# Long convolutions of a Hyena layer: packed outer stages, another order of partition rows, stores on SyncE's queue, loads asked for earlier

## The chip, the cores and the metric

One core of one Trainium2 chip runs the whole program. The metric is the device time of one execution in microseconds (us). Of the kernel before, three executions were timed; one further execution was recorded by the hardware profiler.

## What is computed

The reference is a two-layer backbone over 1024 latent tokens of width 1024 (and 256 context tokens). Layer 0 mixes tokens with a gated linear recurrence, layer 1 with an order-2 Hyena operator; each is followed by a squared-ReLU MLP with 4096 hidden units. The change lies in the Hyena operator of layer 1 alone, which cut to its core is:

```python
def long_conv(u, k_f, bias):
    L = u.shape[1]
    u32 = u.astype(jnp.float32)
    y = jnp.fft.irfft(jnp.fft.rfft(u32, n=2 * L, axis=1) * k_f, n=2 * L, axis=1)[:, :L]
    return (y + u32 * bias).astype(u.dtype)

def hyena_operator(u, p, conv_fn):
    ...
    z = conv_fn(u @ w_in + b_in, conv_w, conv_b, HYENA_CONV_LEFT)
    v, x1, x2 = jnp.split(z, HYENA_ORDER + 1, axis=-1)
    k_f = hyena_filters(L, fw1, fb1, fw2, fb2, fw3, fb3, fw4, freq)
    v = x1 * long_conv(v, k_f[:, 0], skip[0])
    v = x2 * long_conv(v, k_f[:, 1], skip[1])
    return v @ w_out + b_out
```

So there are a projection to three streams with a short convolution along rows of 64 tokens, two long circular convolutions with gates between, and a projection back.

## The kernel before

All work is float32. Weights of the big projections are split into a high and a low part, and three matmuls at a quick format stand for one (L154, L135 to L137). The long convolutions use plain float32 matmuls, which the trace shows as two MATMUL instructions each.

**Projection stage.** `in_gemm` makes 24 blocks of 128 channels. `use` adds the bias (ACT, L888) and does the short convolution (DVE, L894 to L896) for each half of the tokens; `finish`, three blocks later, transposes the blocks of `v` and `x1` (PE, L923; ACT, L924) into `V` and `X1`, or sends a block of `x2` to DRAM (L908).

**The transform.** A long convolution over 1024 tokens padded to 2048 is done as a transform in two stages. The outer forward stage `s1` takes one slice `g` of 8 of `V` and makes two row blocks with two matmuls against `m1` (L864); ACT copies each from PSUM to a tile `e` (L866), and a DMA stores `e` (128 partitions) into 8 partitions of `BIG` (L868), all 16 blocks of them. `prow` says which partitions a row block has. So the stores turn the data by a quarter: `BIG[:, f]` then has all rows of frequency block f on its partitions. Stores are issued by ACT inside the main loop, by SP before it.

**The main loop.** There are four units: two convolutions by two halves of the channels. Each has 16 steps, one for each frequency block. `fstep` loads the filter block `ft` from DRAM (SP, L970), transforms it (PE, L974; ACT copy `kk`, L976), transforms the signal (PE, L979), multiplies them as complex numbers (four DVE operations on half the partitions each, L983 to L986, and for block 0 three small ones more, L989 to L991), and lets POOL add the two products into `y` (L993). `bstep`, three steps later (`LAG`), transforms `y` back (PE, L998) and ACT copies the result over `BIG[:, f]` (L999).

**The outer inverse stage.** `s2p` undoes the outer stage for one slice g: SP loads two row blocks of `BIG` into tiles `e` (L957, pool tag `e2` with six buffers), PE multiplies each by `md` into one PSUM tile (L958), and DVE multiplies by `X1` (L962) or ACT copies (L964) into `V`. The stages `s2p` of unit u-1 and `s1` of unit u+1 ride beside the steps of unit u as a list `side`; from step 4 to step 12 about two entries of it follow each step. In the last unit `back`, which transposes four slices to channels (L1015) and multiplies by `x2` (L1016), takes the place of `s1`.

**Order.** In the main loop `pin` fixes the order of PE's matmuls as written. Elsewhere, and on the other engines, a scheduler that runs with the build sets the order. A wait of an instruction holds back all that stand behind it on the same engine; on SP and ACT that goes for DMA issues too.

**The output projection** follows: `load` fetches weights `hy_w_out`, `gemm2` takes 24 matmuls for each block of 128 channels, and `s2p(3, ...)` and `back(4)` to `back(7)` stand between them.

## Time and profile before

| | |
|---|---|
| Timed executions | 2819.17 us median of 3 (2819.03 to 2819.62) |
| Profiled execution, its own time | 2820.53 us |
| Its span in the profile | 2818.8 us, 30100 instructions |
| PE busy (matmul) | 2664.5 us, 95% of the span |
| DVE, ACT, POOL busy | 1519.5, 1045.7, 256.6 us |

PE is TensorE, DVE VectorE, ACT ScalarE, POOL GpSimd, SP SyncE, which issues most DMAs. PE's share of the span is an average over stages: in most of them it never stops, in the main loop it does.

### The profile page before, as it was taken

The numbers are of one execution on the slowest core, as the hardware profiler recorded it, in microseconds if no ns is written. First come the engines' busy times: TensorE is split into PE (matmuls) and PEld (weight loads), VectorE is DVE, ScalarE is ACT, GpSimd is POOL, SyncE is SP. The second block draws the span as 40 slices with busy tenths as digits, with TensorE's granted clock in tenths as the row PEclk, the third lists the DMA queues.
The fourth block names the chain that finished last, engine by engine and source line by source line (L and its number), as shares of the span: only waits on it lengthen the run. The fifth ranks groups of instructions, "written<-read, shape, count | busy, mean of one in ns | idle before, by whom it ended". The sixth has DMA issues, their size and how long they took to land. (4 is left out here: it accounts for less than half of the span.)

```text
span 2818.8 us, 30100 instructions
## 1 busy us (share of the span) xinstructions
PE 2664.5 (95%) x11578; PEld 2027.9 (72%) x11578; DVE 1519.5 (54%) x2077; ACT 1045.7 (37%) x1566; POOL 256.6 (9%) x162
## 2 busy tenths in 40 slices
PE   6689898999999999999999998889799999999998
PEld 1577777878777777778787763333588888888887
DVE  7665665874554554554843447547485333333336
ACT  5557577552333333322622233323353221112213
POOL 0223333010000000000100013212000000000000
PEclk8789999999999999999999999999999999999999
DMA  8331122342443443431313235555421111111112
GB/s 302 124 123 40 50 75 100 117 129 75 135 134 114 142 133 110 135 114 57 120 56 111 83 123 150 139 162 160 134 83 48 51 47 51 45 53 45 53 45 97
DMA packets 120272, 286.28 MB, mean 102 GB/s; under 512 B 11898, under 2 KB 27900, under 8 KB 120002
## 3 DMA queue, kind: packets, MB, share of 16 engines
q1 hardware_dynamic: 109618, 261.30, 29.5%
q10 hardware_dynamic: 8256, 14.68, 1.8%
q0 software_dynamic: 2256, 8.39, 0.9%
q8 instruction: 91, 1.49, 0.2%
q14 instruction: 51, 0.42, 0.0%
HBM read 212.76 MB, written 37.75 MB: 89 GB/s over the span
## 5 line engine op out<-in xcount | busy, mean ns | idle before, releaser
L154 PE MATMUL ps<-u,whi 128*128 128x512 f32 x2696 | 733.5, 392 | 0.0
L115 ACT CAST whi<-raw 128x1024 fp32r<-128x1024 f32 x206 | 216.7, 1052 | 1130.8 <-PE ps L154 1033.5
L154 PEld LDWEIGHTS ps<-u,whi 128*128 128x128 f32 x2696 | 504.1, 188 | 114.6 <-DVE x L789 4.2
L117 DVE TENSOR_TENSOR wlo<-raw,whi 128x1024 fp32r<-128x1024 f32 x206 | 262.1, 1272 | 468.7 <-ACT whi L115 467.9
L154 PE MATMUL ps<-u,wlo 128*128 128x512 f32 x1348 | 421.3, 389 | 0.1
L154 PEld LDWEIGHTS ps<-u,wlo 128*128 128x128 f32 x1348 | 252.9, 188 | 53.7 <-DVE wlo L117 0.8
L154 PE MATMUL ps<-hh,whi 128*128 128x512 f32 x896 | 290.6, 393 | 0.0
L154 PE MATMUL ps<-hh,wlo 128*128 128x512 f32 x896 | 288.4, 389 | 0.0
L154 PE MATMUL ps<-hl,whi 128*128 128x512 f32 x896 | 287.7, 390 | 0.0
L154 PEld LDWEIGHTS ps<-hh,whi 128*128 128x128 f32 x896 | 168.2, 188 | 51.4 <-DVE x L789 11.1
L136 PE MATMUL ps<-u,whi 128*128 128x512 f32 (+1 forms) x508 | 195.4, 386 | 3.7 <-POOL u L292 3.1
L135 PE MATMUL ps<-u,whi 128*128 128x512 f32 (+1 forms) x508 | 187.3, 385 | 11.5 <-ACT u L291 11.5
L137 PE MATMUL ps<-u,wlo 128*128 128x512 f32 (+1 forms) x508 | 193.1, 382 | 1.8 <-DVE wlo L117 1.8
L154 PEld LDWEIGHTS ps<-hh,wlo 128*128 128x128 f32 x896 | 168.1, 188 | 35.2
L154 PEld LDWEIGHTS ps<-hl,whi 128*128 128x128 f32 x896 | 167.9, 188 | 33.8
L789 DVE SCALAR_TENSOR_TENSOR big<-ps,mod,big 128x512 f32<-128x512 f32 (+1 forms) x132 | 91.7, 731 | 185.2 <-PE ps L154 177.7
L789 DVE SCALAR_TENSOR_TENSOR x<-ps,mod,x 128x512 f32<-128x512 f32 x128 | 91.4, 747 | 132.8 <-PE ps L154 124.9
L415 DVE TENSOR_TENSOR ht<-ps,ht 128x512 f32<-128x512 f32 x64 | 44.0, 687 | 162.9 <-PE ps L137 162.9
L292 POOL TENSOR_TENSOR u<-nu,u 128x512 fp32r<-128x512 f32 x24 | 33.9, 1412 | 990.6 <-ACT u L291 981.4
L135 PEld LDWEIGHTS ps<-u,whi 128*128 128x128 f32 x508 | 98.0, 194 | 30.1 <-ACT u L291 12.3
L136 PEld LDWEIGHTS ps<-u,whi 128*128 128x128 f32 x508 | 98.2, 193 | 25.6 <-POOL u L292 6.4
L137 PEld LDWEIGHTS ps<-u,wlo 128*128 128x128 f32 x508 | 97.7, 192 | 20.3 <-DVE wlo L117 3.0
(228 smaller groups left out, 3798.2 us busy)
## 6 DMA issues: line engine op xcount, KB each, us to landing
raw<-in_mlp_w_dram SPq DMA_DIRECT2D x136, 512.0 KB
adaw<-in_ada_w_dram SPq DMA_DIRECT2D x112, 256.0 KB
fd<-fe SPq DMA_DIRECT2D x64, 256.0 KB
ft<-fd SPq DMA_DIRECT2D x64, 256.0 KB
e<-big SPq DMA_DIRECT2D x64, 256.0 KB
eraw<-in_ada_w_dram SPq DMA_DIRECT2D x24, 512.0 KB
raw<-in_hy_w_in_dram SPq DMA_DIRECT2D x24, 512.0 KB
big<-e ACTq DMA_DIRECT2D x48, 256.0 KB
```

The costliest lines, as they stand in the source:

```text
L115: lsplit[0] = nc.scalar.copy(hi, raw)
L117: lsplit[1] = nc.vector.tensor_tensor(lo, raw, hi.bitcast(F32), op=ALU.subtract)
L135: first = pin(nc.tensor.matmul(ps, wh, rh, start=start, stop=False))
L136: pin(nc.tensor.matmul(ps, wh, rl, start=False, stop=False))
L137: pin(nc.tensor.matmul(ps, wl, rh, start=False, stop=stop))
L154: nc.tensor.matmul(pp[c], x, y[c][k], start=first, stop=last)
L292: applied[k % 2] = (nc.vector if k % 2 else nc.gpsimd).tensor_tensor(ul[k], u, uh[k].bitcast(F32), op=ALU.subtract)
L415: nc.vector.tensor_tensor(ht, ps, ht, op=ALU.mult)
L789: last[0] = nc.vector.scalar_tensor_tensor(xs[m][:, cs], ps[:, :n], g2[:, m:m + 1], xs[m][:, cs], op0=ALU.mult, op1=ALU.add)
```

## The change

Six things change together.

- `s1` and `s2p` take two slices at a time (`gp`). The zero blocks of `m1` and `md` go, and each full matmul becomes several small ones on different parts of the PE array: `s1` 8 matmuls of 32 rows by 64 columns, `s2p` 8 of 64 rows by 32 columns for a pair of slices, where 4 full ones stood. They write to the two single PSUM tiles `st` and `rb` and, for `s1`, to two of the six shared ones.
- For that, tokens lie in another order: `use` permutes in ACT's read and writes the short convolution in five DVE operations with runs of 8 elements where three stood (for `v` and `x1`), `finish` copies the odd slices by quarters of the partitions, two on ACT and two on DVE, and `back` multiplies by a permutation matrix `pm` as a full float32 matmul where it had a transpose.
- `prow` puts neighbouring row blocks into different halves of the partitions.
- All stores of `s1` are issued by SP. In the loop a fourth buffer for `e` is added.
- `s2load` issues the loads of `s2p` apart from it: those of the first two pairs at step 3, with 12 buffers `e2`. In the output projection it stands right ahead of `s2p(3, m)`, with 4 buffers.
- `fload` asks for a filter block three steps ahead, with 4 buffers in place of 8, and `kstep` transforms it one step ahead.

```diff
 def prow(g):
-    return 32 * (g >> 2) + (g & 3)
+
+    return 64 * (g & 1) + 32 * (g >> 3) + (g >> 1 & 3)
...
-            def s1(u, g):
+            def s1(u, gp):
...
-                for m in range(2):
-                    ps = psum()
-                    pin(nc.tensor.matmul(ps, m1[:, m], V[c][:, g], start=True, stop=True))
-                    e = bp.tile([P, 512], F32, tag="e", name=nm("e"), bufs=3)
-                    nc.scalar.copy(e, ps)
-                    b = prow(2 * g + m)
-                    (nc.scalar if cp[0] else nc.sync).dma_start(BIG[u][b:b + 29:4], e)
+                pp = [[psum_st(), psum_rb()], [psum(), psum()]]
+                for r in range(4):
+                    rows = slice(32 * r, 32 * r + 32)
+                    for n in range(2):
+                        k = 3 - r if n else r
+                        pin(nc.tensor.matmul(pp[n][k // 2][64 * (k % 2):64 * (k % 2) + 64], m1[rows], V[c][rows, 2 * gp + n], start=True, stop=True))
+                for n in range(2):
+                    for m in range(2):
+                        if cp[0] and n and m:
+                            e = cp[0].tile([P, 512], F32, tag="e", name=nm("e"), bufs=1)
+                        else:
+                            e = bp.tile([P, 512], F32, tag="e", name=nm("e"), bufs=3)
+                        nc.scalar.copy(e, pp[n][m])
+                        b = prow(4 * gp + 2 * n + m)
+                        nc.sync.dma_start(BIG[u][b:b + 29:4], e)
...
+                    nc.vector.tensor_scalar(ov, zv, cw[:, 1, r:r + 1], cw[:, 3, r:r + 1], op0=ALU.mult, op1=ALU.add)
+                    for tap_, o_, i_ in ((0, ov[:, 1:], zv[:, :7]), (0, ov[:, 0, 1:], zv[:, 7, :7]), (2, ov[:, :7], zv[:, 1:]), (2, ov[:, 7, :7], zv[:, 0, 1:])):
+                        nc.vector.scalar_tensor_tensor(o_, i_, cw[:, tap_, r:r + 1], o_, op0=ALU.mult, op1=ALU.add)
...
-                    nc.scalar.copy(dst[c][:, 4 * g4:4 * g4 + 4, o:o + P], pt.rearrange("p (g d) -> p g d", g=4))
+                    pv = pt.rearrange("p (h n d) -> p n h d", h=2, n=2)
+                    dv = dst[c][:, 4 * g4:4 * g4 + 4, o:o + P].rearrange("p (h n) d -> p n h d", n=2)
+                    nc.scalar.copy(dv[:, 0], pv[:, 0])
+                    for r in range(4):
+                        (nc.scalar.copy if r % 2 else nc.vector.tensor_copy)(dv[96 - 32 * r:128 - 32 * r, 1], pv[32 * r:32 * r + 32, 1])
...
+            def s2load(u, gp, pool=cA, bufs=12):
+
+                ee = rows_[u, gp] = []
+                for n in range(2):
+                    for m in range(2):
+                        e = pool.tile([P, 512], F32, tag="e2", name=nm("e2"), bufs=bufs)
+                        b = prow(4 * gp + 2 * n + m)
+                        nc.sync.dma_start(e, BIG[u][b:b + 29:4])
+                        ee.append(e)
+
+            def s2p(u, gp):
+
                 o, c = units[u]
...
+                po = [psum_st(), psum_rb()]
+                ee = rows_.pop((u, gp))
+                for r in range(2):
+                    rows = slice(64 * r, 64 * r + 64)
+                    for n in range(2):
+                        for m in range(2):
+                            k = 2 * m + r
+                            k = 3 - k if n else k
+                            pin(nc.tensor.matmul(po[n][32 * k:32 * k + 32], md[rows], ee[2 * n + m][rows], start=True, stop=True))
...
+            def fload(i):
+                if i < 64:
+                    fts[i] = cA.tile([P, 512], F32, tag="ft", name=nm("ft"), bufs=4)
+                    nc.sync.dma_start(fts[i], fd[i // 16, FORD[i % 16]])
...
-                        pin(nc.tensor.transpose(pt[:, gg * P:(gg + 1) * P], V[c][:, 4 * g4 + gg, j * P:(j + 1) * P], ident))
+                        pin(nc.tensor.matmul(pt[:, gg * P:(gg + 1) * P], V[c][:, 4 * g4 + gg, j * P:(j + 1) * P], pm[:, gg % 2], start=True, stop=True))
...
+                            def both(u, g):
+                                if g == 0:
+                                    s2load(u, 2)
+                                elif g == 1:
+                                    s2load(u, 3)
+                                s2p(u, g)
+                            side += [lambda g=g, u=u: both(u - 1, g) for g in range(4)]
...
+                    if f == LAG and u:
+                        s2load(u - 1, 0)
+                        s2load(u - 1, 1)
...
                     ys[i] = fstep(u, f)
-                    while len(side) > ns - min(ns, -(-ns * (f - f0 + 1) // (13 - f0))):
+                    fload(i + 3)
+                    if i < 63:
+                        kstep(i + 1)
+                    while len(side) > ns - min(ns, -(-ns * (f - f0 + 1) // (14 - f0))):
```

How the instructions stand is shown at three places. First SP's queue in unit 1, where the row blocks of unit 0 are loaded (L957 before, L990 now, `e`) among the filter blocks (L970 before, L1019 now, `ft`). Before:

```order
L970 DMA ft_12871<-fd 128x512
L957 DMA e_2390_12675<-big_11178 128x1x512
L957 DMA e_2391_12678<-big_11178 128x1x512
L957 DMA e_2394_12684<-big_11178 128x1x512
L957 DMA e_2395_12687<-big_11178 128x1x512
L957 DMA e_2405_12711<-big_11178 128x1x512
L957 DMA e_2406_12714<-big_11178 128x1x512
L970 DMA ft_12910<-fd 128x512
L970 DMA ft_12949<-fd 128x512
L957 DMA e_2408_12719<-big_11178 128x1x512
L957 DMA e_2409_12722<-big_11178 128x1x512
```

The same place of the change, from the sixth of the first run of loads on:

```order
L990 DMA e_2384_12885<-big_11344 128x1x512
L990 DMA e_2385_12887<-big_11344 128x1x512
L990 DMA e_2386_12889<-big_11344 128x1x512
L990 DMA e_2402_12926<-big_11344 128x1x512
L990 DMA e_2403_12928<-big_11344 128x1x512
L990 DMA e_2404_12930<-big_11344 128x1x512
L990 DMA e_2405_12932<-big_11344 128x1x512
L1019 DMA ft_12960<-fd 128x512
L990 DMA e_2417_12966<-big_11344 128x1x512
L990 DMA e_2418_12968<-big_11344 128x1x512
L990 DMA e_2419_12970<-big_11344 128x1x512
L990 DMA e_2420_12972<-big_11344 128x1x512
```

Twelve loads now stand in one run where six stood, one filter block and then the last four follow; the eight filter blocks of steps 0 to 7 are ahead of the run.

Second PE in unit 1, step 4 and after: `s2p` (L958 before, L1004 now), the back transform (L998, now L1055), the filter's (L974, now L1025) and the signal's (L979, now L1036). Before:

```order
L979 MATMUL ps_12664<-big_12181,m_12183 128x512
L958 MATMUL ps_12674<-e_2390_12675,md 128x512
L958 MATMUL ps_12674<-e_2391_12678,md 128x512
L958 MATMUL ps_12683<-e_2394_12684,md 128x512
L958 MATMUL ps_12683<-e_2395_12687,md 128x512
L998 MATMUL ps_12691<-y_12615,mi_12186 128x512
L974 MATMUL ps_12696<-ft_12694,m_12183 128x512
L979 MATMUL ps_12700<-big_12181,m_12183 128x512
```

In the change:

```order
L1025 MATMUL ps_12922<-ft_12866,m_12393 128x512
L1004 MATMUL pst_12934<-e_2379_12875,md 32x512
L1004 MATMUL pst_12934<-e_2380_12877,md 32x512
L1004 MATMUL prb_12935<-e_2381_12879,md 32x512
L1004 MATMUL prb_12935<-e_2382_12881,md 32x512
L1004 MATMUL pst_12934<-e_2379_12875,md 32x512
L1004 MATMUL pst_12934<-e_2380_12877,md 32x512
L1004 MATMUL prb_12935<-e_2381_12879,md 32x512
L1004 MATMUL prb_12935<-e_2382_12881,md 32x512
L1055 MATMUL ps_12947<-y_12845,mi_12396 128x512
L1036 MATMUL ps_12950<-big_12391,m_12393 128x512
L1025 MATMUL ps_12962<-ft_12901,m_12393 128x512
```

Eight small matmuls in a row, which need all four row blocks by the fourth of them, stand where four full ones stood that need one row block each.

Third PE in the output projection (L154 before, L155 now, of `gemm2`), around the third pair of `s2p(3, ...)`. Before:

```order
L154 MATMUL ps_14082<-yh_13976,wlo_14079 128x512
L958 MATMUL ps_14109<-e_2928_14110,md 128x512
L958 MATMUL ps_14109<-e_2929_14113,md 128x512
L958 MATMUL ps_14117<-e_2931_14118,md 128x512
L958 MATMUL ps_14117<-e_2932_14121,md 128x512
L154 MATMUL ps_14125<-yh_13955,whi_14077 128x512
```

In the change:

```order
L1004 MATMUL pst_14431<-e_2927_14423,md 32x512
L155 MATMUL ps_14444<-yh_14264,wlo_14393 128x512
L155 MATMUL ps_14443<-yh_14267,whi_14391 128x512
L1004 MATMUL pst_14431<-e_2928_14425,md 32x512
L1004 MATMUL pst_14431<-e_2927_14423,md 32x512
L1004 MATMUL pst_14431<-e_2928_14425,md 32x512
L1004 MATMUL prb_14432<-e_2929_14427,md 32x512
L155 MATMUL ps_14444<-yh_14270,whi_14391 128x512
L155 MATMUL ps_14443<-v_14247,whi_14391 128x512
L155 MATMUL ps_14444<-v_14247,whi_14391 128x512
L1004 MATMUL prb_14432<-e_2930_14429,md 32x512
```

Here, where no order is fixed, the eight small ones are torn into runs: two runs of four for each of the first two pairs, three runs for the third and four for the fourth, 11 in all.

## Rows read from the trace of the kernel before

**Rows 1.** By stage: length, busy PE, PEld, DVE, ACT, POOL (count), clock, DMA share, GB/s.
```profile
1384.00:1663.00 279.00, 278.46 (x1256) 226.11 (x1255) 119.55 (x174) 82.12 (x129) 8.37 (x9) 1.00 0.21 68
1663.00:1984.00 321.00, 276.53 (x616) 113.85 (x614) 203.28 (x296) 107.99 (x189) 83.82 (x69) 0.95 0.55 160
1984.00:1992.00 8.00, 0.00 (x0) 0.00 (x0) 0.12 (x1) 1.20 (x2) 0.00 (x0) 0.50 0.70 225
1992.00:2056.00 64.00, 63.58 (x259) 46.88 (x260) 33.15 (x43) 26.14 (x36) 0.00 (x0) 0.97 0.39 129
```

**Rows 2.** Timeline of POOL's additions: start, length, operation, idle before and releaser.
```profile
1668.60 1.26 POOL L993 TENSOR_TENSOR y<-t,t 128x512 f32<-128x512 f32 x1 [2.34 <-DVE t L986]
...
1727.82 1.27 POOL L993 TENSOR_TENSOR y<-t,t 128x512 f32<-128x512 f32 x1 [1.55 <-DVE t L986]
1730.65 1.27 POOL L993 TENSOR_TENSOR y<-t,t 128x512 f32<-128x512 f32 x1 [1.56 <-PE ps L974]
...
1777.21 1.27 POOL L993 TENSOR_TENSOR y<-t,t 128x512 f32<-128x512 f32 x1 [10.35 <-DVE t L990]
...
1817.50 1.28 POOL L993 TENSOR_TENSOR y<-t,t 128x512 f32<-128x512 f32 x1 [1.56 <-DVE t L986]
...
1873.59 1.27 POOL L993 TENSOR_TENSOR y<-t,t 128x512 f32<-128x512 f32 x1 [7.45 <-DVE t L990]
...
1912.13 1.27 POOL L993 TENSOR_TENSOR y<-t,t 128x512 f32<-128x512 f32 x1 [1.55 <-DVE t L986]
...
1950.62 1.27 POOL L993 TENSOR_TENSOR y<-t,t 128x512 f32<-128x512 f32 x1 [8.12 <-DVE t L990]
...
1980.17 1.26 POOL L993 TENSOR_TENSOR y<-t,t 128x512 f32<-128x512 f32 x1 [1.56 <-DVE t L986]
```

**Rows 3.** Timeline of SP's loads and of the matmuls that wait for them.
```profile
1730.40 5.76 SPq L957 DMA_DIRECT2D e<-big  x6
...
1734.47 1.10 PE L958 MATMUL ps<-e,md 128*128 128x512 f32 x2 [0.43 <-DMA e<-big]
1736.28 1.12 PE L958 MATMUL ps<-e,md 128*128 128x512 f32 x2 [0.72 <-DMA e<-big]
1738.31 1.10 PE L958 MATMUL ps<-e,md 128*128 128x512 f32 x2 [0.90 <-DMA e<-big]
...
1820.33 5.70 SPq L957 DMA_DIRECT2D e<-big  x6
...
1913.75 5.69 SPq L957 DMA_DIRECT2D e<-big  x6
```

**Rows 4.** Busy time in three short stretches (columns as in rows 1).
```profile
1668.00:1680.00 12.00, 11.36 (x27) 4.51 (x25) 8.71 (x13) 2.93 (x5) 5.06 (x4) 1.00 0.98 350
...
1732.00:1738.00 6.00, 4.26 (x9) 1.17 (x7) 5.86 (x9) 1.17 (x2) 2.54 (x2) 1.00 0.54 144
...
2002.00:2006.00 4.00, 4.00 (x20) 3.30 (x19) 1.17 (x2) 4.00 (x6) 0.00 (x0) 1.00 0.52 192
```

**Rows 5.** Chain that ended last, in the output projection: start, length, what.
```profile
2009.03 3.43 PE ps L958 x8
...
2048.39 0.87 PE ps L1015 x8
```

**Rows 6.** Timeline of PE in the filter stage, small matmuls among full ones.
```profile
913.68 1.09 PE L432 MATMUL ps<-ht,mf 32*32 32x512 f32 x16
...
914.70 0.50 PE L154 MATMUL ps<-hh,whi 128*128 128x512 f32 x1
```

**Rows 7.** Timeline of ACT's copies ahead of the stores, unit 1.
```profile
1787.66 0.59 ACT L866 COPY e<-ps 128x512 f32<-128x512 f32 x1 [1.44 <-DMA big<-e]
1789.64 0.59 ACT L866 COPY e<-ps 128x512 f32<-128x512 f32 x1 [1.39 <-DMA big<-e]
```

**Rows 8.** Timeline of the first store of unit 0 and the transfer ahead of it.
```profile
1665.71 0.54 POOL L908 DMA_DIRECT2D x2d<-zo  x1 [0.68 <-DVE zo L896]
...
1676.77 2.98 ACTq L868 DMA_DIRECT2D big<-e  x3
```

More of the change, by code (lines that the diff above doesn't have):

```diff
@@ L896, in use, with done @@
                 nc.vector.scalar_tensor_tensor(ov[:, :, :63], zv[:, :, 1:], cw[:, 2, r:r + 1], ov[:, :, :63], op0=ALU.mult, op1=ALU.add)
+                done(m, c)
+            def done(m, c):
                 if c == 1:
@@ L949, in load_mi @@
                 nc.gpsimd.dma_start(mi[q], a["mi"][:, 4 * q:4 * q + 4])
-            def s2p(u, g):
-                o, c = units[u]
-                po = psum()
-                for m in range(2):
-                    e = cp[0].tile([P, 512], F32, tag="e2", name=nm("e2"), bufs=6)
-                    b = prow(2 * g + m)
-                    nc.sync.dma_start(e, BIG[u][b:b + 29:4])
-                    pin(nc.tensor.matmul(po, md[:, m], e, start=(m == 0), stop=(m == 1)))
-                if o == 0:
-                    if g == 0:
-                        V[c] = vtile()
-                    nc.vector.tensor_tensor(V[c][:, g], po, X1[c][:, g], op=ALU.mult)
-                else:
-                    nc.scalar.copy(V[c][:, g], po)
+            rows_ = {}
@@ new lines, in s2load @@
+            def s2load(u, gp, pool=cA, bufs=12):
[7 more added lines that the diff above has]
+            def s2p(u, gp):
+                o, c = units[u]
+                po = [psum_st(), psum_rb()]
[7 more added lines that the diff above has]
+                            pin(nc.tensor.matmul(po[n][32 * k:32 * k + 32], md[rows], ee[2 * n + m][rows], start=True, stop=True))
+                if o == 0 and gp == 0:
+                    V[c] = vtile()
+                for n in range(2):
+                    g = 2 * gp + n
+                    if o == 0:
+                        nc.vector.tensor_tensor(V[c][:, g], po[n], X1[c][:, g], op=ALU.mult)
+                    else:
+                        nc.scalar.copy(V[c][:, g], po[n])
@@ new lines, in hyena, with kstep @@
+            kks, fts = {}, {}
+            def fload(i):
+                if i < 64:
+                    fts[i] = cA.tile([P, 512], F32, tag="ft", name=nm("ft"), bufs=4)
+                    nc.sync.dma_start(fts[i], fd[i // 16, FORD[i % 16]])
+            def kstep(i):
+                j, ft = i % 16, fts.pop(i)
+                pk = psum()
+                pin(nc.tensor.matmul(pk, m2[j // 4][:, j % 4, 64:192], ft, start=True, stop=True))
+                kk = cpool.tile([P, 512], F32, tag="kk", name=nm("kk"), bufs=3)
+                nc.scalar.copy(kk, pk)
+                kks[i] = kk
@@ L1026, in hyena @@
             pinned[0] = True
+            for i in range(3):
+                fload(i)
+            kstep(0)
             for i in range(64 + LAG):
@@ L1037, in hyena @@
                         if u > 0:
-                            side += [lambda g=g, u=u: s2p(u - 1, g) for g in range(8)]
+                            def both(u, g):
[5 more added lines that the diff above has]
+                            side += [lambda g=g, u=u: both(u - 1, g) for g in range(4)]
                         if u < 3:
-                            side += [lambda g=g, u=u: s1(u + 1, g) for g in range(8)]
+                            side += [lambda g=g, u=u: s1(u + 1, g) for g in range(4)]
                         else:
@@ L1100, in hyena @@
                 if m < 4:
-                    s2p(3, 2 * m)
-                    s2p(3, 2 * m + 1)
+                    s2load(3, m, cp[0], 4)
+                    s2p(3, m)
                 else:
@@ L1260, in _consts @@
     p = np.arange(P)
-    gm = 4 * (p >> 5) + (p & 3)
+    gm = (p >> 6) + 8 * (p >> 5 & 1) + 2 * (p & 3)
     q = (p >> 2) & 7
```

57 lines of the change are left out of this document (32 added, 25 removed).

## Prediction

> **What bounds the kernel now.** I first cut the Hyena layer into stages and read each engine's busy time and the clock there [rows 1]. In the projection (1384 to 1663 us) PE is busy 278.5 of 279 us at full clock: what leaves PE there is gained whole. In the main loop PE is busy 276.5 of 321 us, DVE 203, and neither ends all the steps. Then come 8 us without PE, in which the clock stands at 0.50, the lower of its two levels (1.2 GHz), and the output projection, where PE is busy 63.6 of 64 us.
>
> For the loop I read the timeline of POOL's addition, which closes each step [rows 2]. Undisturbed steps are 2.83 us apart (1727.82 to 1730.65), four DVE operations of 0.7; sixteen would make 45.3 us. The units take 59.2 (1668.60 to 1727.82), 89.7, 94.6 and 68.1 us. So some 14, 44, 49 and 23 us per unit go to waits. The loads in unit 1 show which [rows 3]: SP issues six at 1730.40, PE's matmuls for them start at 1734.47, 1736.28 and 1738.31, each after a wait for the load. One row block of 256 KB comes every 1.92 us, the first 4.07 after its issue. Those loads use half of the DMA engines: 0.54 of them are busy at 144 GB/s, where the loop's start reaches 0.98 and 350 [rows 4]. The stores are alike: three buffers, each copy of ACT waits for a store, and the copies are 1.98 us apart [rows 7]. The change alters neither the 8 partitions on one side of these transfers nor their size.
>
> **The matmuls.** Two slices of an outer stage are four full matmuls, eight instructions, 3.43 us when nothing waits [rows 5]. What stands in their place is not in the trace, but the filter stage has its like: 16 instructions, eight small float32 matmuls of 32 by 32 on different parts of the array, start at 913.68, and the next full matmul at 914.70 [rows 6]: 1.02 us. The bounds are 1.02, all eight at once, and 6.86, one after another (8 x 0.857, a quarter of the 3.43). I take 1.02, since these tiles too lie on eight different parts. A pair then saves 2.41.
>
> The row also bears on a rule. There, four row groups write into one PSUM tile at the same time, and the eight still end in 1.02. The Trainium skill (TensorEngine Tiling (Array Packing), section Gotcha 1: PSUM Pressure) says that different row tiles cannot access the same PSUM bank simultaneously. `s1` and `s2p` write each bank from two row groups; by the rule their pairs would take two rounds. No wait of that sort shows in the row.
>
> **Projection stage.** Four pairs of `s1` on a saturated PE: 4 x 2.41, -9.6. The added work lies on DVE and ACT: for 16 blocks, two small DVE operations for each half of the tokens, and in each of two copies one whole ACT copy becomes a half one and four quarters, two of them on DVE. That is 64 + 64 DVE operations and 64 more of ACT. If each took as long as a DVE operation of the loop (0.7) and as ACT's copy of a whole tile (0.59, rows 7), it would be 90 and 38 us; DVE has 119.6 and ACT 82.1 busy of 279 [rows 1]. So they are hidden behind PE. Without that cover, at the end of the stage, up to 8 DVE copies stand before the first step: at most 5.6 us, at least nothing; I take +2.
>
> **Unit 0.** The first store must wait until the last block of `x2` has left: POOL issues that at 1665.71, and the first store goes at 1676.77 [rows 8]. That stays; now the store waits on SP, and behind it the filter blocks from number 6 on and the second pair of stores. The fourth buffer and pairs at steps 0, 3, 7 and 10 leave time enough for all later stores. 45.3, some 1.4 estimated for the three small operations of block 0, and 6 for that one wait: 52.7 for 59.2, -6.5.
>
> **Units 1 to 3, the loads.** Asked for at the same moment as now, since they need the last back transform of the unit before. SP's order shows twelve in one run, a filter block, then four. The first group may start when the fourth block has landed, so PE stops for each group, in order, and DVE behind it. The 16th block is ready at 4.07 + 15 x 1.92 + 0.7 for the filter block = 33.6 us after the issue; then one packed group (1.0), a back and a signal transform (1.7), a step of DVE (2.8) and block 0's small operations (1.4): step 8 closes after 40.5. Now it takes 46.8 in unit 1 (1730.40 to 1777.21), 53.3 in unit 2, where the four `x2` transfers stand among the loads, and 36.9 in unit 3 [rows 2, 3]. So -6.3, -12.8 and +3.6. Asking ahead ends the round trips through six buffers, not the 1.92.
>
> **Units 1 and 2, the stores.** Four pairs at steps 9 to 12. The first finds free buffers; each of three later ones waits until the four stores before it and a filter block are through: 3 x (4 x 1.9 + 0.7) = 24.9, and four steps of 2.83 around: 36.2 from step 8 to the next unit. Now it is 40.3 and 38.5 [rows 2]: -4.1 and -2.3. In unit 3 `back` follows, one a step, with two more DVE operations each: 7 x 2.83 + 4 x 1.4 = 25.4 for 29.6, -4.2. Issue by SP in place of ACT is costed at nothing: ACT's copies wait for the stores themselves, and filter blocks asked for three steps ahead cover SP's wait. PE has less to do in the loop and may fall to the lower clock more often; it waits there anyway.
>
> **Output projection.** The 16 full matmuls (13.7) become small ones, but torn into 11 runs, and a run costs at least one matmul's 0.86: I take 0.9, 9.9 in all, -3.8. `back(4)` to `back(7)`: eight transposes take 0.87 [rows 5]; a full float32 matmul of 128 columns is a quarter of 0.857, eight are 1.7: 4 x 0.85, +3.4. With four buffers the loads of pair m+1 start only when pair m is done; a block here comes every 1.37 us (256 KB at 192 GB/s, rows 4), so four need 8.2 with the first's lead of 4.07, against about 7 us of other matmuls: +2 for two pairs. Together +1.6. The 8 idle us stay.
>
> **Sum.** -9.6 + 2 - 6.5 - 10.4 - 15.1 - 0.6 + 1.6 = -38.6. The profiled execution took 2820.5, so 2781.9; it lies 1.4 above the median of the timed ones, and I forecast **2780.5 us**.
>
> **The rivals.** Under 0.2% (5.6 us) a measurement of this kernel can't tell from no change.
>
> 1. Forecast: loads stay at 1.92. Chance 0.45.
> 2. *Loads and stores run at 1.37.* In the output projection the same loads, with the same half of the engines, move 192 GB/s and not 144 [rows 4]. Something in the loop slows them; if it is neighbours that meet in the same partitions, the new `prow` ends it. Then 16 x 0.55 = 8.8 less per unit, 26 us, and for the stores 3 x 4 x 0.5 = 6 per unit, 12: 2743. Against it: the loads in the output projection are in the old order too, and fast. 0.20.
> 3. *The loop gains nothing*, since the same 32 transfers per unit go through the same half of the engines and the new order only shifts the waits: only -9.6 + 1.6 remain, 2811. 0.13.
> 4. *Groups of stores don't overlap*, since SP takes stores and filter blocks in one order: three buffers at 1.98 make 5.9 us for one round now; a group alone would then take 5.9 + 3 x 1.9 = 11.6 in place of 8.3, nine groups: +30, of which the spread groups of unit 0 hide a third: 2800. 0.09.
> 5. *Two rounds on PSUM.* A second round is at least 0.86 a group, on the path for the four of the projection and some of the output projection, and once a unit: +8, 2789. By the Trainium skill's rule on PSUM banks, above, this would be the case. The row of the filter stage speaks against it [rows 6]. 0.05.
> 6. *Slower: DVE becomes the bound of the projection.* The short convolution now writes runs of 8 elements with gaps. Such a form is not in the trace. It concerns 96 of DVE's 174 instructions there, by their share 66 of 119.6 us [rows 1]. At three times their length, and with the added operations at their bound, DVE would need 119.6 + 132 + 90 = 342 of 279: +63, 2843. It decides from about 2.6 times on, where the excess eats the whole gain. Against it: these forms touch no more elements than the old ones. 0.08.
>
> **Range.** It reaches from rival 2 to rival 3: 2742 to 2812; outside lie the slow case and the lower half of rival 2. **Faster** by over 0.2%: cases 1, 2, 4, 5 and three quarters of 3, 0.88; **within**: the rest of 3, 0.04; **slower**: 0.08.
>
> **What would show it.** PE's rows of the packed groups: eight small matmuls in about 1.0 us from start to the next start. In the loop, POOL's additions: 2.83 apart in steps 0 to 3 and 13 to 15, 7.7 apart in steps 5 to 8 with PE waiting for loads, about 8 in steps 10 to 12 with ACT waiting for stores. If the spacing in steps 5 to 8 is near 5.5, it is rival 2; if DVE is busy all through the projection, rival 6. The forecast fails if the transfers' rate isn't what I read, or if a wait on SP's queue that I cost at nothing ends a step.

## The result, and the profile after

The changed kernel takes 2792.24 us (median of 4 runs, 2787.97 to 2794.38) where the kernel before takes 2819.1 on the same chip: a ratio of 0.9904, with a 95% interval of 0.9887 to 0.9921. The forecast was 2780.5 with a range of 2742 to 2812: the direction and the range hold, and of the 38.6 us forecast about 27 came. The profiled execution took 2791.55 us, its span is 2789.8 (before 2818.8).

First the busy time by stage, in the columns of [rows 1], for the kernel after.

```profile
1384.00:1653.24 269.24, 268.08 (x1286) 218.68 (x1284) 148.85 (x289) 94.98 (x183) 8.65 (x10) 1.00 0.22 71
1653.24:1662.00 8.76, 4.22 (x6) 1.64 (x6) 6.88 (x16) 4.95 (x14) 1.86 (x4) 0.81 0.97 352
1662.00:1947.00 285.00, 251.17 (x823) 89.76 (x822) 197.75 (x290) 101.69 (x181) 79.47 (x63) 0.92 0.57 167
1947.00:1955.00 8.00, 2.25 (x4) 0.59 (x4) 1.73 (x3) 1.17 (x2) 1.60 (x2) 0.78 0.61 216
1955.00:2027.00 72.00, 69.49 (x322) 45.41 (x323) 33.91 (x43) 27.43 (x37) 0.00 (x0) 0.93 0.40 122
```

The projection is shorter, and PE still sets it: DVE has 148.85 of 269 us, so rival 6 is out. A gap that was not there before stands behind it (PE 4.22 busy of 8.76). In the loop neither PE (251 of 285) nor DVE (198) is full, and the clock has fallen to 0.92.

Next POOL's additions that close steps 0, 16, 32, 48 and 63, as in [rows 2].

```profile
1664.54 1.28 POOL L1050 TENSOR_TENSOR y<-t,t 128x512 f32<-128x512 f32 x1 [5.26 <-PE ps L1036]
...
1712.79 1.27 POOL L1050 TENSOR_TENSOR y<-t,t 128x512 f32<-128x512 f32 x1 [1.56 <-DVE t L1043]
...
1788.13 1.27 POOL L1050 TENSOR_TENSOR y<-t,t 128x512 f32<-128x512 f32 x1 [2.47 <-DVE t L1043]
...
1874.42 1.27 POOL L1050 TENSOR_TENSOR y<-t,t 128x512 f32<-128x512 f32 x1 [2.31 <-DVE t L1043]
...
1948.90 1.26 POOL L1050 TENSOR_TENSOR y<-t,t 128x512 f32<-128x512 f32 x1 [1.56 <-DVE t L1043]
```

The units take 48.3, 75.3, 86.3 and 74.5 us, for 59.2, 89.7, 94.6 and 68.0 before. Unit 1 gains 14, more than forecast; unit 2 gains 8, about half of what was forecast; unit 3 loses 6.

PE's timeline in the projection shows what a packed group costs (the first and the last of its 16 instructions, and the full matmul behind it).

```profile
1521.30 0.64 PE L871 MATMUL pst<-v,m 32*64 32x512 f32 x1
...
1521.83 0.59 PE L871 MATMUL ps<-v,m 32*64 32x512 f32 x1
1522.35 1.20 PE L155 MATMUL ps<-u,whi 128*128 128x512 f32 x4
```

From 1521.30 to 1522.35 is 1.05 us for 16 instructions, where the forecast took 1.02. Two row groups write into each PSUM tile in that time, each into 64 partitions of its own, so the second round of rival 5 does not exist. The Trainium skill (TensorEngine Tiling (Array Packing), section Gotcha 1: PSUM Pressure) says that different row tiles cannot access one PSUM bank simultaneously; here the trace does not show the wait that this would make.

SP's timeline shows when the row blocks of units 1 to 3 are asked for, and what stands among them.

```profile
1714.68 10.12 SPq L990 DMA_DIRECT2D e<-big  x12
...
1792.57 10.41 SPq L990 DMA_DIRECT2D e<-big  x12
...
1806.12 6.70 SPq L990 DMA_DIRECT2D e<-big  x4
...
1818.38 0.80 SPq L1063 DMA_DIRECT2D v<-x2d  x2
...
1824.09 3.16 SPq L1063 DMA_DIRECT2D v<-x2d  x2
...
1878.86 10.34 SPq L990 DMA_DIRECT2D e<-big  x12
```

Four short stretches of the kernel after, columns as in [rows 4]: stores of unit 2, loads of unit 2, loads of unit 3, and loads in the output projection.

```profile
1844.00:1868.00 24.00, 19.04 (x63) 6.37 (x62) 13.86 (x21) 11.73 (x22) 6.64 (x6) 1.00 0.60 198
...
1793.00:1811.00 18.00, 14.69 (x46) 3.91 (x44) 10.19 (x15) 2.93 (x5) 3.80 (x3) 0.81 0.56 142
...
1897.00:1914.00 17.00, 14.11 (x54) 3.85 (x44) 5.50 (x8) 4.47 (x8) 2.94 (x3) 0.80 0.63 161
...
1990.00:1993.00 3.00, 3.00 (x15) 2.45 (x14) 0.04 (x1) 0.69 (x2) 0.00 (x0) 1.00 0.53 201
```

With much the same share of the DMA engines (0.53 to 0.63), the loads in the loop move 142 and 161 GB/s, the stores 198, the loads in this stretch of the output projection 201. A DMA moves its data in packets; one of 2 KB takes 127 ns on average in both stretches of loads in the loop, 99 in the stores (median 84) and 85 in the output projection. Rival 2 is out as far as the loads go: the new `prow` did not end the slow ones. Its figure for the stores, 1.37 us a block, is near what they now take (256 KB at 198 GB/s are 1.3), though not by `prow` (e3).

That the loads keep their old rate shows in PE's waits too. In unit 2 the first matmuls of the first four row blocks start 1.91 to 1.94 us apart, where the forecast had 1.92 (unit 1: 1.83 to 1.84; unit 3: 1.92 to 1.94).

```profile
1796.52 1.04 PE L1004 MATMUL pst<-e,md 64*32 64x512 f32 x2 [0.30 <-DMA e<-big]
1798.43 1.04 PE L1004 MATMUL pst<-e,md 64*32 64x512 f32 x2 [0.87 <-DMA e<-big]
1800.37 1.10 PE L1004 MATMUL prb<-e,md 64*32 64x512 f32 x2 [0.89 <-DMA e<-big]
1802.30 1.06 PE L1004 MATMUL prb<-e,md 64*32 64x512 f32 x1 [0.83 <-DMA e<-big]
```

### The profile page after: what moved, and what is told of

Read it like the earlier page. It is cut to its first block, busy times and chain, and to the rows that moved or that the text cites. A ratio compares the mean times of both kernels' runs of the same rounds, so it can differ in the third digit from the quotient of the medians.

```text
span 2789.8 us, 30962 instructions
## 1 busy us (share of the span) xinstructions
PE 2639.5 (95%) x11898; PEld 1995.4 (72%) x11898; DVE 1552.9 (56%) x2205; ACT 1059.4 (38%) x1630; POOL 255.9 (9%) x162
## 4 chain that ended last, share of the span: by engine, by line
PE 70%; DMA 5%; DVE 4%; ACT 1%; issue 1%; SPq 1%; POOL 0%; DVEq 0%; ACTq 0%; POOLq 0%
PE ps L155 55%; DMA e<-big 3%; PE ps L137 3%; PE ps L138 3%; PE ps L136 3%; DMA big<-e 1%; PE ps L433 1%; PE ps L1055 1%; PE ps L1025 1%; PE ps L1036 1%; SPq L990 1%; PE prb L1004 0%; DVE nt L289 0%; PE ps L949 0%; DVE o L1321 0%
## 5 line engine op out<-in xcount | busy, mean ns | idle before, releaser
L155 PE MATMUL ps<-u,whi 128*128 128x512 f32 x2696 | 730.1, 391 | 0.0
L155 PEld LDWEIGHTS ps<-u,whi 128*128 128x128 f32 x2696 | 503.6, 188 | 114.8 <-DVE x L790 4.2
L155 PE MATMUL ps<-u,wlo 128*128 128x512 f32 x1348 | 420.4, 389 | 0.1
L155 PEld LDWEIGHTS ps<-u,wlo 128*128 128x128 f32 x1348 | 252.9, 188 | 53.5 <-DVE wlo L118 0.8
L155 PE MATMUL ps<-hh,whi 128*128 128x512 f32 x896 | 290.5, 393 | 0.0
L155 PE MATMUL ps<-hh,wlo 128*128 128x512 f32 x896 | 288.4, 389 | 0.0
L155 PE MATMUL ps<-hl,whi 128*128 128x512 f32 x896 | 287.7, 390 | 0.0
L155 PEld LDWEIGHTS ps<-hh,whi 128*128 128x128 f32 x896 | 168.2, 188 | 51.4 <-DVE x L790 11.1
L136 PE MATMUL ps<-u,whi 128*128 128x512 f32 (+1 forms) x508 | 186.9, 384 | 11.8 <-ACT u L292 11.5
L155 PEld LDWEIGHTS ps<-hh,wlo 128*128 128x128 f32 x896 | 168.1, 188 | 35.2
L155 PEld LDWEIGHTS ps<-hl,whi 128*128 128x128 f32 x896 | 167.8, 188 | 33.9
```

Source lines behind the costliest of these rows:

```text
L136: first = pin(nc.tensor.matmul(ps, wh, rh, start=start, stop=False))
L155: nc.tensor.matmul(pp[c], x, y[c][k], start=first, stop=last)
```

## The experiments

All are the changed kernel with one edit. The part ahead of the projection is the same in all, but it ends at 1404.7 to 1409.0 us, so stages are compared and not absolute times. The runs come from several chips, on which the kernel before takes 2816.3 to 2819.1 us; each ratio is to the kernel before on the same chip, and differences of medians are good to some 3 us. The table has, in us: from the first matmul of line 155 (154 before) to DVE's first operation of the loop; units 0 to 3, by the first operation of steps 0, 16, 32, 48 and 63; from there to the end of the span; and the median of the timed runs.

| kernel | projection | unit 0 | unit 1 | unit 2 | unit 3 | rest | median |
|---|---|---|---|---|---|---|---|
| before | 259.9 | 59.2 | 89.7 | 94.6 | 68.0 | 841.6 | 2819.1 |
| after | 256.9 | 48.3 | 75.3 | 86.3 | 74.5 | 843.8 | 2792.2 |
| e1 loads of 128 partitions | 256.7 | 48.4 | 62.9 | 63.7 | 56.7 | 839.3 | 2737.9 |
| e2 x2 behind unit 3's loads | 256.6 | 48.5 | 76.7 | 80.3 | 80.6 | 844.5 | 2795.5 |
| e3 old `prow` | 256.9 | 49.1 | 78.2 | 85.8 | 75.4 | 842.8 | 2795.7 |
| e4 half of the loads by POOL | 256.9 | 49.1 | 77.3 | 82.0 | 72.8 | 845.6 | 2793.8 |
| e5 four row-block buffers | 256.8 | 48.3 | 90.0 | 98.9 | 87.2 | 846.2 | 2837.7 |
| e6 filter blocks not ahead | 256.7 | 51.1 | 84.0 | 86.2 | 75.7 | 843.1 | 2808.3 |
| e7 stores by ACT | 257.0 | 52.0 | 79.7 | 88.2 | 76.8 | 844.8 | 2803.8 |
| e8 X1 earlier | 256.7 | 50.5 | 78.2 | 85.7 | 76.0 | 842.8 | 2797.4 |
| e9 x2 ahead of unit 3's loads | 256.7 | 48.4 | 74.1 | 85.6 | 76.3 | 847.4 | 2794.7 |
| e10 rows through DRAM | 256.7 | 52.0 | 81.9 | 91.5 | 79.3 | 848.7 | 2819.0 |
| e11 groups twice | 260.3 | 48.5 | 81.9 | 84.8 | 74.8 | 845.7 | 2807.1 |
| e12 one copy for four | 250.8 | 54.0 | 79.4 | 85.2 | 71.0 | 840.7 | 2789.5 |

e2, e8 and e9, which leave unit 1 alone, have 76.7, 78.2 and 74.1 there for 75.3: a unit by itself is good to some 3 us.

### Is it the row blocks' loads? (e1, e4, e5, e10)

```diff
-nc.sync.dma_start(e, BIG[u][b:b + 29:4])
+nc.sync.dma_start(e, BIG[u][:, FORD[15]])
```

> The changed kernel, but each of the 64 loads of a row block reads 128 partitions of BIG (the block of the last back transform, 2 KB of each partition) in place of 8 partitions of 32 KB: the same bytes, the same two memories, released by the same back transform. The rows that come are the wrong ones; nothing else is left out. Theory (a transfer with 8 partitions on one side uses half of the DMA engines, and this is what steps 5 to 8 of units 1 to 3 wait for): a block then takes about 0.75 us (256 KB at the 350 GB/s of the loop's start) in place of 1.9, and step 8 closes 22 to 28 us after the loads' issue, with PE or DVE as the bound, in place of 42.3, 50.5 and 44.8: 14, 22 and 20 us less, the output projection some 2 to 5 less: 2725 to 2745. Rival (something else in the loop, the engines' own accesses or the lower clock, holds the blocks at 1.7 us or more): 2782 to 2792, with packets as slow as before.

Measured: 2737.88 us, 54 less than after (ratio to before 0.9717, 0.9701 to 0.9733). The gain lies in units 1 to 3 (12.4, 22.6, 17.8). The theory holds: these loads are what the loop waits for. Columns as in [rows 4]:

```profile
1724.00:1728.00 4.00, 4.00 (x18) 1.35 (x18) 3.88 (x7) 0.58 (x1) 1.44 (x2) 1.00 1.03 382
```

All DMA engines are at work (1.03) and move 382 GB/s. The Trainium skill (DMA: Bandwidth & Descriptors, section Why a DMA increments its semaphore by 16 and not by 1) says that the sizes of the slowest dimensions on both sides set how many engines a DMA takes; shares of 0.53 with 8 partitions and 1.03 with 128 agree. But it is not the count of engines alone:

```diff
-nc.sync.dma_start(e, BIG[u][b:b + 29:4])
+(nc.gpsimd if m else nc.sync).dma_start(e, BIG[u][b:b + 29:4])
```

> The changed kernel, with every second load of a row block issued by POOL and the others by SP as before. Theory (half of the engines is the bound, and POOL's transfers can take the other half): two blocks are under way at a time, 16 come in about 16 to 18 us in place of 31, and steps 5 to 8 of units 1 to 3 lose 10 to 13 us each: 2753 to 2765. Rival 1 (POOL's transfers use the same half): 2790 to 2796. Rival 2 (POOL's issue delays its additions, which close every step): about 1 us for each of 8 loads in a unit, 24 in all, 2800 and more.

Measured: 2793.81 us, the time of rival 1, but not for its reason (columns as above):

```profile
1728.00:1734.00 6.00, 1.67 (x4) 0.00 (x0) 0.00 (x0) 0.00 (x0) 0.00 (x0) 0.50 1.08 172
```

POOL's transfers do take the other half of the engines (share 1.08), yet together they move 172 GB/s, a fifth more than one half alone (142). With twice the engines a packet of 2 KB takes 194 ns on average, half as long again. DVE, ACT and POOL compute nothing in that stretch and PE little, so it is not their work that slows the loads.

```diff
-def s2load(u, gp, pool=cA, bufs=12):
+def s2load(u, gp, pool=cA, bufs=4):
...
-if g == 0:
-    s2load(u, 2)
-elif g == 1:
-    s2load(u, 3)
+if g:
+    s2load(u, g)
 s2p(u, g)
...
-    s2load(u - 1, 1)
```

> The changed kernel with four e2 buffers in the loop in place of twelve: each group's four row blocks are asked for when the group before it is done, as in the output projection. It asks why a 2 KB packet of these loads takes 119 to 126 ns in the loop and 84 to 86 in the output projection, with the same partitions and sizes. Theory (more than four blocks under way at a time slow each other down): packets return to 84 to 90 ns, some 94 per us, a group takes 4.07 + 3 x 1.37 + 1 = 9.2 us, and the time stays at 2785 to 2793 although nothing is asked ahead. Rival (something else in the loop slows them, whatever the number): 119 to 126 ns again, 4.07 + 3 x 1.92 + 1 = 10.8 us a group, some 4 to 8 us more in each of units 1 to 3, 2800 to 2815.

Measured: 2837.73 us, slower than the kernel before (1.0075, 1.006 to 1.0091). The rival holds as to the packets: they take 125 ns with four blocks under way too, and the stretch below moves 129 GB/s while PE and ACT mostly wait. The size was off: each group also pays the 4 us from issue to first block (1716.81 to 1720.78 for the first) and waits at the lower clock (0.65 in the stretch below), and the first halves of units 1 to 3 grow by 15.2, 12.3 and 12.7. So asking for twelve blocks at once is worth some 45 us; with four buffers the loop takes 324 us in all, more than the 312 before the change.

```profile
1724.00:1727.00 3.00, 1.45 (x2) 0.18 (x2) 2.05 (x3) 0.00 (x0) 1.44 (x2) 0.65 0.53 129
```

```diff
+bd = [dram.tile([16, P, 512], F32, name=f"bd{k}") for k in range(4)]
...
-nc.sync.dma_start(e, BIG[u][b:b + 29:4])
+nc.sync.dma_start(e, bd[u][:, b:b + 29:4].rearrange("f q c -> q f c"))
...
 nc.scalar.copy(BIG[u][:, FORD[j]], ps)
+nc.scalar.dma_start(bd[u][FORD[j]], BIG[u][:, FORD[j]])
```

> The changed kernel with each back transform's block of 256 KB stored to DRAM also (issued by ACT, 128 partitions on one side), and the row blocks loaded from there: the same 2 KB packets, the same eight DMA engines and the same order at the e2 tiles, but no 8 partitions of SBUF as the source. Theory (the 8 source partitions are what holds a packet at 126 ns): 84 to 100 ns, a block each 1.35 to 1.6 us, steps 5 to 8 of units 1 to 3 lose 5 to 9 us each and gain about 2 for the trip through DRAM: 2772 to 2785. Rival (the eight engines or the writing end): 120 ns and more, the trip on top, 2794 to 2806.

Measured: 2818.98 us, beyond both ranges. The packets come out as the theory has it: 86 ns each, 97 per us, 199 GB/s with half of the engines, into the same tiles.

```profile
1733.00:1740.00 7.00, 6.51 (x17) 1.51 (x18) 1.29 (x2) 0.00 (x0) 0.00 (x0) 0.52 0.52 199
```

The time falls on the rival's side for another reason: the loads are issued at 1726.54, 9.5 us into unit 1 in place of 4.8, since a filter block more stands ahead of them on SP and waits for its buffer, and then the last store to DRAM holds them for 0.6 us; and 64 more transfers of 256 KB pass among the stores, whose halves of units 1 and 2 grow from 35.5 to 40.9.

### Which rows, who issues, what stands ahead (e3, e7, e6)

```diff
-return 64 * (g & 1) + 32 * (g >> 3) + (g >> 1 & 3)
+return 32 * (g >> 2) + (g & 3)
...
-gm = (p >> 6) + 8 * (p >> 5 & 1) + 2 * (p & 3)
+gm = 4 * (p >> 5) + (p & 3)
```

> The changed kernel with the old order of partitions in BIG (prow and the matching order of the constants). Theory (what a row block costs depends on its 8 partitions, not on which of them): loads 1.9 us, stores as after, 2789 to 2795. Rival (the new order is what made the stores quick, 198 GB/s in place of 162): the stores fall back to 1.98 us, 3 x 4 x 0.45 us in each of units 1 and 2, some 11 in all, 2800 to 2806.

Measured: 2795.74 us; the interval of its ratio, 0.9906 to 0.9936, overlaps that of after. The second halves of units 1 and 2 take 36.0 and 36.3 for 35.5 and 35.7. The order of partitions gains nothing that can be told here, and is not what made the stores quick.

```diff
-nc.sync.dma_start(BIG[u][b:b + 29:4], e)
+(nc.scalar if cp[0] else nc.sync).dma_start(BIG[u][b:b + 29:4], e)
```

> The changed kernel with the stores of the loop issued by ACT, as before the change, in place of SP. Theory (ACT's copies wait for the stores themselves, and who issues them costs nothing): 2788 to 2797, and the stores as quick as after, near 198 GB/s. Rival (on SP they stand behind filter blocks, or ahead of them): the second halves of units 1 and 2, 35.5 us from step 8 on, change by more than 3 us each, in either direction.

Measured: 2803.79 us, 11.5 more than after (13 by the sum of the stages); the interval of its ratio, 0.9939 to 0.9968, does not overlap that of after. Unit 0 grows by 3.7, the second halves of units 1 and 2 by 2.1 and 2.2: under the 3 us of the rival's bound, but all in its direction. Who issues the stores does cost something, 8 us in these three places.

```diff
-for i in range(3):
-    fload(i)
-kstep(0)
...
+fload(i)
+kstep(i)
 ys[i] = fstep(u, f)
-fload(i + 3)
-if i < 63:
-    kstep(i + 1)
```

> The changed kernel with each filter block asked for, multiplied and copied in its own step, as before the change, in place of three steps (the load) and one step (the matmul and ACT's copy) ahead. Theory (the waits of units 1 to 3 are for row blocks and stores, so that filter blocks asked ahead gain nothing there): 2789 to 2797. Rival (in each step that follows a wait, DVE then also waits for the filter's load, matmul and copy, 0.86 + 0.6 us or more): at least 16 such steps, 2815 and more.

Measured: 2808.31 us, between the two expectations. Unit 0 gives back 2.8 and unit 1 8.7; units 2 and 3 stay. So filter blocks asked ahead are worth some 16 us by the medians (12 by the stages), and the theory is wrong to give them nothing.

### Does x2 make unit 2 long? (e2, e9)

The four loads of x2 are put behind unit 3's row blocks (e2), and ahead of them behind unit 2's last stores (e9):

```diff
 v = vtile()
-for ct in range(4):
-    gate(ct, v[:, 2 * ct:2 * ct + 2].rearrange("p a b -> p (a b)"))
...
 elif g == 1:
     s2load(u, 3)
+if u == 2 and g == 1:
+    for ct in range(4):
+        gate(ct, v[:, 2 * ct:2 * ct + 2].rearrange("p a b -> p (a b)"))
 s2p(u, g)
```

> The changed kernel, with the four loads of x2 (512 KB each) asked for behind the sixteen row blocks of unit 3 and no longer among those of unit 2. Theory (in unit 2 they share the DMA engines with the last row blocks): step 8 of unit 2 closes some 42 us after the loads' issue as in unit 1, not 50.5, and the time is 2783 to 2786. Rival (the lower clock of PE sets unit 2, or the late transfers now hold the first back): at most 2 us from unit 2, or unit 3 longer by as much: 2790 to 2795.

```diff
-nc.sync.dma_start(BIG[u][b:b + 29:4], e)
+lst.append(nc.sync.dma_start(BIG[u][b:b + 29:4], e))
...
+with tc.issue_after(lst[-1].ins), tc.issue_after(lst[-2].ins):
     for ct in range(4):
         gate(ct, v[:, 2 * ct:2 * ct + 2].rearrange("p a b -> p (a b)"))
```

> The changed kernel with the four loads of x2 asked for behind the last four stores of unit 2, ahead of unit 3's row blocks: in the 14 us in which only filter blocks are loaded. Theory (x2 costs what it takes from the row blocks it meets, 5.6 us in unit 2, and as much in unit 3 where it was put behind its row blocks): step 8 of unit 2 closes 5 to 6 us earlier, unit 3 stays, 2785 to 2789. Rival (the 6 us of x2 now delay filter blocks or the last stores): nothing gained, 2791 and more.

Measured: 2795.52 and 2794.69 us, no gain from either. In e2 unit 2 loses 6.0 and unit 3 gains 6.1: the x2 transfers cost what they take from the row blocks they meet, wherever that is. In e9 the first half of unit 2 is 2.5 shorter, its second half 1.8 longer and unit 3 1.8 longer. Both rivals hold: where transfers are the bound, moving one moves the wait.

### The front of the loop (e8, e12)

PE and ACT at the end of the projection, in the kernel after:

```profile
1650.46 2.78 PE L949 MATMUL ps<-ident,zo 128*128 128x128 f32 x24
1657.78 2.02 PE L1025 MATMUL ps<-ft,m 128*128 128x512 f32 x2 [4.54 <-ACT v L954]
...
1655.02 0.69 ACT L954 COPY v<-ps 32x256 f32<-32x256 f32 x2 [0.72 <-DVE v L954]
1656.58 1.49 ACT L954 COPY v<-ps 32x256 f32<-32x256 f32 x4 [0.86 <-DVE v L954]
1658.92 0.37 ACT L954 COPY v<-ps 32x256 f32<-32x256 f32 x1 [0.86 <-DVE v L954]
```

The first matmul of the loop waits 4.54 us for a PSUM tile that the copies of the last three blocks still hold, and then takes 2.02 for two instructions in place of 1.02, at the lower clock (0.54 granted from 1657.70 to 1659.90). The copies of 32 partitions wait for one another in turn (ACT for DVE, in each row).

```diff
-order = list(range(15)) + list(range(16, 24)) + [15]
+order = list(range(14)) + list(range(16, 24)) + [14, 15]
...
-if m == 14:
+if m == 13:
     s1(0, 3)
```

> The changed kernel with two blocks of x2, not one, as the last of the projection, so that one block of X1 (8 transposes, 10 copies) and not three (24 transposes, 30 copies) is left behind its last matmul. Theory (the loop's first matmul waits 4.5 us for PSUM tiles that these copies hold, and then finds the lower clock): the first step of the loop comes 4 to 5 us earlier, 2786 to 2789. Rival (the wait only passes on to the later transfer of x2, behind which the first row stores and filter blocks stand): less than 1.5 us earlier, 2790 to 2795.

Measured: 2797.36 us, and the loop's first step comes 0.2 us earlier: the rival, 2 us above its range.

```diff
-for r in range(4):
-    (nc.scalar.copy if r % 2 else nc.vector.tensor_copy)(dv[96 - 32 * r:128 - 32 * r, 1], pv[32 * r:32 * r + 32, 1])
+nc.scalar.copy(dv[:, 1], pv[:, 1])
```

> The changed kernel with one ACT copy of 128 partitions in place of the four copies of 32 partitions (two of DVE, two of ACT) that follow each set of four transposes. The reversal of rows in every second slice is left out by that, and nothing else. Theory (the copies of three blocks, in turn on ACT and DVE, hold the loop's first step back; costed at 2 us, they take 6): from the first matmul of the projection's long run to the first DVE operation of the loop it takes 251 to 253 us in place of 256.9, and the time is 2786 to 2788. Rival (the first step waits for a transfer or for the lower clock anyway): 255.5 or more, 2790 to 2795.

Measured: 250.8 us to the first step, 6.1 less, as the theory has it; but 2789.47 us, within the intervals of after. Unit 0 takes 54.0 for 48.3. ACT's timeline there:

```profile
1667.74 0.59 ACT L878 COPY e<-ps 128x512 f32<-128x512 f32 x1 [6.05 <-DMA x2d<-zo]
```

Now ACT waits 6.05 us for the last block of x2 to leave: the wait of [rows 8]. The end of unit 0 stays where it was (256.9 + 48.3 = 305.2, and 250.8 + 54.0 = 304.8).

### What the packing is worth (e11)

The same is done in `s2p`.

```diff
 for r in range(4):
     ...
         pin(nc.tensor.matmul(pp[n][k // 2][64 * (k % 2):64 * (k % 2) + 64], m1[rows], V[c][rows, 2 * gp + n], start=True, stop=True))
+for r in range(4):
+    ...
+        pin(nc.tensor.matmul(pp[n][k // 2][64 * (k % 2):64 * (k % 2) + 64], m1[rows], V[c][rows, 2 * gp + n], start=True, stop=True))
```

> The changed kernel with the matmuls of every packed group issued twice (the second writes the same results over the first). A group costs 1.0 us; 4 stand in the projection, 12 of s1 and 12 of s2p in the loop, 4 in the output projection. Theory (the packing pays where PE is the bound, and in the loop PE waits for transfers anyway): 4.2 us more in the projection, about 4 in the output projection, 0 to 5 in the loop, 2800 to 2806. Rival (PE's time in the loop is on the path, since it wakes at the lower clock): each of the 24 groups adds 1 us or more, 24 to 35 us more there, 2825 to 2835.

Measured: 2807.11 us, 15 more. The projection takes 3.4 more and the rest 1.9 more. The 24 us of added work in the loop lengthen unit 1 by 6.6, of which some 3 are scatter, and the other units not at all. The theory holds, 1 us above its range and 18 below the rival's: packing pays in the projection, and in the loop PE's time is hidden behind the transfers.

## Why the prediction was right in direction and short in size

**Projection, -9.6: right.** From the first matmul of line 155 (1404.71) to the end of the last transposes (1653.24) is 248.5 us; before it was 258.0 (1405.77 to 1663.80). That is -9.5. The lines are after's first one, its last ones being shown above (L949), then before's first and last.

```profile
1404.71 1.20 PE L155 MATMUL ps<-u,whi 128*128 128x512 f32 x4
...
1405.77 1.20 PE L154 MATMUL ps<-u,whi 128*128 128x512 f32 x4
...
1660.94 2.86 PE L923 MATMUL ps<-ident,zo 128*128 128x128 f32 x24
```

**Front of the loop, +2, and unit 0, -6.5: right as a sum, both wrong in size.** The first step comes 8.3 us behind the last transposes, for 1.9 before: +6.4, more than the forecast's bound of 5.6. That bound counted 8 copies of DVE at 0.7 us; there are 12 of 0.41, in turn with 12 of ACT of 0.36, and PE starts at the lower clock behind the wait. Unit 0 gains 10.9. Together -4.5, as the forecast's two terms make. The forecast counted the wait for x2 inside unit 0 at 6 us; e12 shows that the late first step simply stands in place of that wait.

**Units 1 to 3, the mark.** The forecast's terms end where POOL's addition closes step 8, block 0's step. By that mark it took 42.3, 50.5 and 44.8 us from the loads' issue, for 40.5 forecast. But in the changed kernel DVE does step 9's four products ahead of block 0's last small operation (1756.36 in unit 1), and the additions of steps 8 and 9 follow each other by 1.2 us. So the first operation of step 8 is the fairer mark, and the table's. The forecast's sum puts it 33.6 + 1.0 + 1.7 = 36.3 us behind the issue. Measured: 35.0, 43.2 and 37.5, for 42.3, 48.8 and 32.4 before (three lines of after, one of the small operation, three of before).

```profile
1749.69 0.68 DVE L1040 TENSOR_TENSOR t<-ps,kk 64x512 f32<-64x512 f32 x1 [0.72 <-PE ps L1036]
...
1835.78 0.68 DVE L1040 TENSOR_TENSOR t<-ps,kk 64x512 f32<-64x512 f32 x1 [2.87 <-PE ps L1036]
...
1916.37 0.68 DVE L1040 TENSOR_TENSOR t<-ps,kk 64x512 f32<-64x512 f32 x1 [2.95 <-PE ps L1036]
...
1756.36 0.48 DVE L1047 MEMSET t<- 1x512 f32 x1 [0.16 <-DVE t L1043]
...
1772.72 0.68 DVE L983 TENSOR_TENSOR t<-ps,kk 64x512 f32<-64x512 f32 x1 [3.23 <-PE ps L979]
...
1869.11 0.68 DVE L983 TENSOR_TENSOR t<-ps,kk 64x512 f32<-64x512 f32 x1 [2.33 <-PE ps L979]
...
1946.12 0.68 DVE L983 TENSOR_TENSOR t<-ps,kk 64x512 f32<-64x512 f32 x1 [5.04 <-PE ps L979]
```

**Unit 1, -10.4: measured -14.4.** Up to step 8 it gained 8.0 (6.3 forecast), behind it 6.3 (4.1 forecast). The second term was mis-sized: it gives 8.3 us to each of three groups of stores, and ACT's four groups of copies start 4.8, 7.3 and 6.4 us apart (the last two are shown). Stores do not take 1.9 us for a block but, at 198 GB/s, 1.3. Against that stands a wait that the forecast put at nothing: PE waits 1.78 us for a filter block, which SP asks for only behind the last stores (1778.29). Which part of the change made the stores quicker is open; it is not `prow` (e3), and the issuing engine (e7) explains 2 us a unit. The fourth buffer for `e`, which no run takes away, is a candidate that was not tested.

```profile
1766.14 0.59 ACT L878 COPY e<-pst 128x512 f32<-128x512 f32 x1 [0.43 <-DMA big<-e]
...
1772.54 0.59 ACT L878 COPY e<-pst 128x512 f32<-128x512 f32 x1 [0.42 <-DMA big<-e]
...
1783.96 1.10 PE L1036 MATMUL ps<-big,m 128*128 128x512 f32 x2 [1.78 <-DMA ft<-fd]
```

**Unit 2, -15.1: measured -8.3.** The step that failed is "the 16th block is ready at 4.07 + 15 x 1.92 + 0.7": the rate of 1.92 held, the count of blocks did not. It gave one filter block to the sixteen row blocks and nothing to x2, which it had itself named as what makes this unit long. Between the first row packet and the last one of the unit the trace moves 18.9 blocks of 256 KB in unit 1 (1715.5 to 1746), 23.2 in unit 2 (1793.5 to 1830, of which 3.8 are x2) and 19.7 in unit 3 (1880 to 1914). A filter block can be asked for whenever a buffer comes free, and x2 as soon as its tile is free, and all pass through the same engines. The last group of unit 2 so ends at 1831.6, 39 us after the issue, where the forecast had 34.6; and PE, having waited, starts again at the lower clock (0.81 and 0.80 in the two rows of loads in the section on the result). e2 and e9 show that x2 could not have gone anywhere free of charge.

```profile
1830.51 1.07 PE L1004 MATMUL prb<-e,md 64*32 64x512 f32 x2
```

**Unit 3, -0.6: measured +6.4.** Here the blocks are not the main error: step 8 starts 37.5 us behind the issue, 1.2 above the forecast. As forecast, the loads go as soon as the last back copy ends. But that is now 7.4 us behind DVE's first operation of units 2 and 3, where it was 5.8 and 4.6 (unit 1: 4.8 for 5.5), so part of what a unit gains at its end is lost at the start of the next. In e6, without filter blocks asked ahead, it is 4.6 and 4.1. And the back matmuls at unit 3's end gained 1.5 by the table's mark and not 4.2.

**Output projection, +1.6: measured +2.3 for all that follows the loop.** In the chain that ended last (start, length, what) the first wait for row blocks is 6.70 us, a group is 0.99, and each of the four `back` is 1.78, where a transpose group was 0.87 [rows 5] and the forecast had 1.7.

```profile
1952.67 6.70 DMA e<-big
...
1965.20 10.20 PE ps L155 x44
1975.40 0.99 PE pst L1004 x8
...
2003.37 1.78 PE ps L1072 x16
```

**What was costed at nothing.** Issue by SP in place of ACT is worth some 11 to 13 us (e7), and filter blocks asked ahead 12 to 16 (e6); both are gains that the forecast had put down to other terms or left out. That the sum came out only 10 to 12 us from the measured one owes something to such errors of both signs.

**Summed up:** -1.1 ahead of the projection (the scatter named above), -9.5, -4.5, -14.4, -8.3, +6.4 and +2.3 are -29.1; the spans differ by 29.0.

## What to carry to other kernels

Where transfers bound a stage, count every transfer that may pass in it, also those that a scheduler can pull forward, and not only the ones that are waited for: moving x2 twice moved the wait and not the time. Two waits that end at the same moment are one term: a stall removed ahead of an older wait gives nothing (e12). Packing pays where PE is the bound (9.5 us for four pairs in the projection), and asking ahead pays where it waits (45 us for row blocks), so the two have to be costed apart. No run with the whole computation beats the changed kernel; what could is a layout in which a row block lies in all 128 partitions, up to 54 us by e1, if it can be had for less.
